# A delta-net projection that takes its input before the norm factor is known: where the factor is applied, and when waiting banks are evacuated

## The chip, the core and the metric

The kernel runs on one core of a Trainium2 chip. The metric is the device time of one execution in microseconds (us). Engines are named as in the profile: PE (TensorE's matmuls), PEld (its weight loads), DVE (VectorE), ACT (ScalarE), POOL (GpSimd), SP (SyncE, here a queue of DMAs); "q" behind a name is the engine's sequencer.

## The reference

The model has 256 tokens of width 1024 and two blocks. Only the first layer of the first block matters here:

```python
h = h + gated_deltanet(rmsnorm(h, a_norm_w), a_w_in, ...)
h = h + conv_gated_mlp(rmsnorm(h, ffn_norm_w), ...)
# gated_deltanet(hn, ...):
proj = hn @ w_in                      # q, k (8 heads), v, z (16 heads) of 128, gates b and a
qkv = silu(causal_dwconv(qkv, conv_w))        # width 4
q, k = l2norm(q) * 128**-0.5, l2norm(k)
beta = sigmoid(b); g = -exp(a_log) * softplus(a + dt_bias)
o = chunked_gated_delta_rule(q, k, v, g, beta)
o = rmsnorm(o, out_norm_w) * silu(z)
return o @ w_out
```

`rmsnorm` multiplies each token's row by its own factor (the inverse root of the mean square) and each column by a weight. The factor is one number for a token, so it can be applied to the input of a product or to its result.

## The kernel before, in words

One builder writes the whole program; a scheduler then orders each engine's instructions, the older ones first where several are ready. Activations lie transposed, 128 features by 256 tokens a tile. Each fp32 operand is split into a high and a low part, and each product of two tiles is three matmuls (`mm3`, lines 247 to 251): input high with weight high, input low with weight high, input high with weight low.

**Weights.** They lie in DRAM as 362 chunks of eight 128x128 tiles, in the order of use. `_raw` (line 168) loads a chunk through SP's queue, `_prep` (line 175) makes its high part on ACT (L186) and its low part on DVE (L187). `w` (line 230) hands out a tile, prepares two chunks ahead and, at every fourth tile, calls `tick`, which lets each waiting side task take one step. So a step is four tiles or twelve matmuls; side tasks count their delays in steps (`yield`).

**PSUM.** There are eight banks. `gemm` (line 257) fills a bank with two output tiles; with `ko=2` the first two banks are filled together, going through the eight input tiles once. A full bank goes to `evac` (line 207), which evacuates at once if `ready`, else keeps it in `evq`.

**The delta-net stage** (`gdn`, line 547, and `gdn_body`, line 576). The head loads the input in four parts (L519), squares it on ACT (L557), sums (L502, L558, L366), makes the factor (`rstd`, L379 and on), spreads it over a PSUM bank (`rows`, L418), and multiplies input, weight and factor on DVE (L568) before the split (L569, L570). `warm` (L554) puts products without use on PE in between. Weight chunk 0 is prepared meanwhile, chunks 1 and 3 behind given tiles of the input (`PINS`, through `behind`, line 192, which fixes an order on an engine).

Then the projection is multiplied: the first two banks of keys, the gates (`w_ba`, evacuated by `evac_ba`, line 609), two more banks of keys, and then blocks in the order of `ORDER` = "qqzqqzvvvvvvzvvz", where q is a bank of queries, v one of values, and z two banks of the output gate. In step numbers the keys end in step 18 and the last block in step 98.

- `conv` (line 646) evacuates a bank of k, q or v: for each of its two tiles one op on ACT (L651) and three on DVE (L654), then silu on ACT (L655). They read the bank itself.
- Nine steps later the squares of k or q are summed over features into bank `ssb` (L673).
- `x_stage` (line 701) waits for all four sums of keys and the gates, computes factors on DVE (`factors`, line 681), and then makes for eight pairs of heads key products (L707), decays (L711 to L715) and their product (L716); eight DMAs for each half (L722) take the result to DRAM.
- `inv_stage` (line 751) loads it back (L756) and inverts 32x32 blocks in 31 steps of two DVE ops (L764, L766), then sends results round again (L772 to L779).
- `levels` (line 865) joins the blocks to whole inverses (y1, z1, y2, z2), starting ten steps after the inversion with y1p (L832). `chain(q4)` (line 879) makes four heads' output: y0, x10, y1, o0, o1, then factor and gate on DVE (L929 to L937), a transpose (L945) and a split (L435, L436).
- The output projection `acc_k` adds up over 16 heads as they come.

Each of these is a side task; where the program has to wait for one without tiles to multiply, `until` (line 225) runs steps without products between them.

**Elsewhere.** `stats` (line 384) already does in the later norms what the change does here: the product starts, and the factor is applied at evacuation (L995 in the FFN). In `ffn2` (line 1685) `self.pins` holds the low parts of two chunks behind the DVE op that makes `dgx` (L1746), on which the products of L1760 depend.

Of the kernel before, what the change touches and what calls it, by code (L numbers as in the profile page):

```python
# [9 lines left out]
F32 = mybir.dt.float32  # L10
# [102 lines left out]
WARM = (5, 1, 3)  # L113
# [7 lines left out]
WSSB = 9  # L121
# [11 lines left out]
PRE0 = 1  # L133
# [5 lines left out]
PINS = {1: 0, 3: 1}  # L139
ORDER = "qqzqqzvvvvvvzvvz"  # L140


class Builder:
# [31 lines left out]
    def _prep(self, j):  # L175
# [12 lines left out]
        if j in self.pins:  # L188
            self.behind(i, self.pins[j])
# [67 lines left out]
    def gemm(self, name, x, K, ctiles, evac, ko=0):  # L257
# [170 lines left out]
    def split(self, hi, lo, src, scale=None, eng=None):  # L428

        nc = self.nc  # L430
        if scale is None:
            nc.scalar.activation(hi, src, AF.Copy)
            nc.vector.tensor_tensor(lo, src, hi.bitcast(F32), ALU.subtract)
# [71 lines left out]
    def run(self):  # L505
        nc, tc = self.nc, self.tc
        with ExitStack() as es:
# [9 lines left out]
            self.ident = self.cp.tile([P, P], F32, name="ident")  # L517
            for b in range(4):
# [4 lines left out]
            self.ones = self.cp.tile([P, P], F32, name="ones")  # L523
            nc.gpsimd.memset(self.ones, 1.0)
# [22 lines left out]
    def gdn(self):  # L547
# [3 lines left out]
        with tc.tile_pool(name="gp", bufs=1) as gp:  # L551

            wb = self.bank("warm")
            warm = lambda n, r: [nc.tensor.matmul(wb[:, 0 : r.shape[1]], self.ones, r, start=True, stop=True) for _ in range(n)]  # L554
            warm(WARM[0], self.ones)
            for b in range(4):
                self.add_sq(self.sqs, "sqa", b, lambda o: nc.scalar.activation(o, self.h[:, 2 * b : 2 * b + 2], AF.Square))  # L557
            nc.vector.tensor_tensor(self.sqs[0], self.sqs[0], self.sqs[1], ALU.add)  # L558
            cs = self.colsum(self.sqs[:1])
            if PRE0:  # L560
                self._prep(0)
            rc = self.rstd(cs, D)
            warm(WARM[1], self.sqs[0])
            rb = self.rows(rc, psum=True)
            warm(WARM[2], self.h[:, 0])
            for i in range(8):
                t = gp.tile([P, T], F32, tag="t2", bufs=8, name="xn")
# [8 lines left out]
    def gdn_body(self, gp, x):  # L576
# [32 lines left out]
        def evac_ba(g, b):  # L609
# [24 lines left out]
            def later():  # L634
                for _ in range(6):
                    yield
# [1324 lines left out]
```

## Time and profile before

| | us |
|---|---|
| median of three runs | 1212.6 (1211.88 to 1213.06) |
| the profiled execution, its own time | 1211.13 |
| its span, first to last instruction | 1209.3 |
| PE busy in the span | 1185.4 |
| DVE busy | 890.1 |
| ACT busy | 686.7 |

The profile is one execution. A row of a timeline gives the start, the length, engine and line, what is written from what, how often the instruction came in a row, and in brackets how long its engine was idle before it and what ended that. A row of groups gives busy time and the mean of one; matmuls overlap, so their pace is read from counts in a stretch, not from the mean. A row of windows gives for each engine its busy time and number of instructions in a stretch, then the granted clock's share, the DMA engines' share and GB/s.

### The profile page before, as it was taken

Reading aid. Unit: us, or ns where it says so; the run is one execution under the profiler, and the core shown is the slowest. Engines: PE = TensorE matmul, PEld = TensorE weight load, DVE = VectorE, ACT = ScalarE, POOL = GpSimd, SP = SyncE. Lnnn points to the kernel's source line nnn. Section 1 sums busy time; section 2 is a strip of 40 time slices with the busy share of each in tenths; the row PEclk is TensorE's granted clock in tenths of the full one; section 3 lists DMA queues with packets and bytes.
Section 4 is the critical chain, followed back from the end, with each engine's and each line's share of the span. In section 5 each row is a group of like instructions: output and inputs, shape, how many; then the busy total and the mean of one; then the engine's idle time right before and its main releaser. Section 6 shows DMA issues by size and latency. Waiting matters only on the chain.

```text
span 1209.3 us, 23369 instructions
## 1 busy us (share of the span) xinstructions
PE 1185.4 (98%) x9368; PEld 1122.7 (93%) x9368; DVE 890.1 (74%) x1642; ACT 686.7 (57%) x1166; POOL 20.4 (2%) x47
## 2 busy tenths in 40 slices
PE   6999999999999999999999999999999999999997
PEld 6989988999999999989999999889799999999996
DVE  6968977668877778879977878756656567655555
ACT  4786556556655556556655556754465455444443
POOL 1000000000000001000000000000000000000000
PEclk9999999999999999999999999999999999999999
DMA  6546385454655557434655655363255563555552
GB/s 212 187 134 201 120 223 178 140 165 155 208 187 180 188 178 248 131 102 149 206 185 184 192 183 165 116 201 123 88 174 175 176 241 119 180 185 184 188 181 82
DMA packets 68205, 206.00 MB, mean 170 GB/s; under 512 B 18086, under 2 KB 18230, under 8 KB 67841
## 3 DMA queue, kind: packets, MB, share of 16 engines
q1 hardware_dynamic: 65488, 194.77, 50.3%
q0 software_dynamic: 2608, 9.75, 2.3%
q8 instruction: 73, 1.20, 0.4%
q14 instruction: 36, 0.29, 0.1%
HBM read 199.75 MB, written 4.74 MB: 169 GB/s over the span
## 4 chain that ended last, share of the span: by engine, by line
PE 92%; DVE 5%; ACT 2%; issue 1%; DMA 0%; SPq 0%; DVEq 0%; ACTq 0%
PE pb L249 21%; PE pb L250 20%; PE pb L251 20%; PE acc L249 7%; PE acc L251 7%; PE acc L250 7%; DVE wl L187 1%; PE pt L1163 1%; PE ssb L673 1%; DMA ident<-cst 0%; DVE cy L654 0%; PE kv L1567 0%; ACT wh L186 0%; PE y1p L903 0%; PE csum L366 0%
## 5 line engine op out<-in xcount | busy, mean ns | idle before, releaser
L187 DVE TENSOR_TENSOR wl<-wr,wh 128x1024 fp32r<-128x1024 f32 x362 | 442.0, 1224 | 200.0 <-ACT wh L186 198.6
L186 ACT ACTIVATE wh<-wr 128x1024 fp32r<-128x1024 f32 x362 | 381.7, 1056 | 335.8 <-issue 99.3
L249 PE MATMUL pb<-xh,wh 128*128 128x256 f32 x1224 | 347.7, 284 | 0.6 <-ACT xh L569 0.6
L251 PE MATMUL pb<-xh,wl 128*128 128x256 f32 x1224 | 345.5, 283 | 0.7 <-DVE wl L187 0.7
L250 PE MATMUL pb<-xl,wh 128*128 128x256 f32 x1224 | 345.3, 282 | 0.2 <-DVE xl L570 0.2
L249 PEld LDWEIGHTS pb<-xh,wh 128*128 128x128 f32 x1224 | 231.6, 189 | 2.7 <-issue 1.3
L250 PEld LDWEIGHTS pb<-xl,wh 128*128 128x128 f32 x1224 | 230.3, 188 | 0.5 <-DVE xl L570 0.4
L251 PEld LDWEIGHTS pb<-xh,wl 128*128 128x128 f32 x1224 | 229.5, 188 | 0.9 <-DVE wl L187 0.9
L249 PE MATMUL pb<-fh,wh 128*128 128x256 f32 x416 | 118.4, 285 | 0.0
L250 PE MATMUL pb<-fl,wh 128*128 128x256 f32 x416 | 117.5, 283 | 0.1
L251 PE MATMUL pb<-fh,wl 128*128 128x256 f32 x416 | 116.7, 281 | 0.0
L249 PE MATMUL acc<-ah,wh 128*128 128x256 f32 x352 | 98.7, 280 | 0.0
L251 PE MATMUL acc<-ah,wl 128*128 128x256 f32 x352 | 98.6, 280 | 0.0
L250 PE MATMUL acc<-al,wh 128*128 128x256 f32 x352 | 98.5, 280 | 0.0
L249 PEld LDWEIGHTS pb<-fh,wh 128*128 128x128 f32 x416 | 77.9, 188 | 1.4 <-issue 0.4
L250 PEld LDWEIGHTS pb<-fl,wh 128*128 128x128 f32 x416 | 78.2, 188 | 1.1 <-DVE fl L436 0.3
L251 PEld LDWEIGHTS pb<-fh,wl 128*128 128x128 f32 x416 | 78.9, 190 | 0.0
L1002 DVE SCALAR_TENSOR_TENSOR fy<-fpad,cols,fy 128x256 f32<-128x256 f32 x176 | 73.6, 479 | 0.0
L249 PE MATMUL pb<-wh,xh 128*128 128x512 f32 (+1 forms) x176 | 70.3, 401 | 0.0
L250 PE MATMUL pb<-wl,xh 128*128 128x512 f32 (+1 forms) x176 | 68.2, 388 | 1.1 <-DVE wl L187 1.1
L251 PE MATMUL pb<-wh,xl 128*128 128x512 f32 (+1 forms) x176 | 67.9, 386 | 0.0
L249 PEld LDWEIGHTS acc<-ah,wh 128*128 128x128 f32 x352 | 66.8, 190 | 0.0
(438 smaller groups left out, 2082.7 us busy)
## 6 DMA issues: line engine op xcount, KB each, us to landing
wr<-wall SPq DMA_DIRECT2D x362, 512.0 KB, 3.6
wzd<-zt POOLq DMA_DIRECT2D x8, 256.0 KB, 2.9
wzog<-wzd POOLq DMA_DIRECT2D x4, 512.0 KB, 4.0
bias<-bd POOLq DMA_DIRECT2D x4, 512.0 KB, 7.4
h<-xT SPq DMA_DIRECT2D x4, 256.0 KB, 4.1
h<-xT POOLq DMA_DIRECT2D x1, 1024.0 KB, 7.6
wrow<-wrow POOLq DMA_DIRECT2D x1, 1024.0 KB, 9.0
out_dram<-mw SPq DMA_DIRECT2D x4, 256.0 KB, 2.0
```

The lines of the kernel that those rows point to most:

```text
L186: nc.scalar.activation(hi, r, AF.Copy)
L187: i = nc.vector.tensor_tensor(lo, r, hi.bitcast(F32), ALU.subtract)
L249: mm(out, ah, bh, start=start, stop=False, skip_group_check=skip)
L250: mm(out, ah, bl, start=False, stop=False, skip_group_check=skip)
L251: mm(out, al, bh, start=False, stop=stop, skip_group_check=skip)
L673: nc.tensor.matmul(ssb[:, c : c + 1], sq[:, i, tt * P : tt * P + P], self.ones[:, 0:1], start=True, stop=True)
L1002: nc.vector.scalar_tensor_tensor(y[:, i], u[:, i, j : j + T], w(j), y[:, i], ALU.mult, ALU.add)
L1163: nc.tensor.transpose(pt[:, j * P : j * P + P], S[:, i, j * P : j * P + P], self.ident)
```

## The change

- The input is split with its norm weight alone, as its parts land; the factor is made in a side task (`norm`) during the projection and applied at evacuation: by a new DVE op in `conv` (bank times row factor into `un`) and in `evac_ba`, and as the scale of z's copy.
- Banks wait in `evq` until the factor is there (step 14), and are then taken one every `NE` = 4 steps. The new op in `conv` is ordered behind the latest low part of weights on DVE.
- In the head input parts and weight chunks alternate on SP's queue; ident moves to POOL's queue, the norm weights come alone on ACT's, cols come last. ACT's and DVE's ops of the head are chained in written order. Thirteen products without use run ahead on PE.
- With `ko`, the products of one input tile are ordered by kind: all with both high parts, all with the input's low part, all with the weights' low part. This holds for all `gemm` calls with `ko`.
- A z block comes first in `ORDER`; delays of side tasks change; `x_stage`'s factors get a higher priority and three steps more; four of its last eight stores go to ACT's queue.
- `_prep` no longer looks into `self.pins`; `ffn2` still fills it.

```diff
-WARM = (5, 1, 3)
+WARM = 13
+NE = 4
+NA1, NA2 = 9, 4
-WSSB = 9
+WSSB = {"kss": 7, "qss": 9}
-PINS = {1: 0, 3: 1}
-ORDER = "qqzqqzvvvvvvzvvz"
+ORDER = "zqqzqqvvvvvvzvvz"
...
-        if j in self.pins:
-            self.behind(i, self.pins[j])
+        self.lastwl = i
...
             for k in range(K):
+                ts = []
                 for g in range(ko):
                     for i, c in enumerate(groups[g]):
-                        wh, wl = self.w(name, k * P, c * P)
-                        self.mm3(banks[g][:, i * T : i * T + T], wh, wl, xh[:, k], xl[:, k],
-                                 k == 0 and i == 0, k == K - 1, True)
+                        ts.append((banks[g][:, i * T : i * T + T], *self.w(name, k * P, c * P), k == 0 and i == 0))
+                for o, wh, wl, first in ts:
+                    mm(o, wh, xh[:, k], start=first, stop=False, skip_group_check=True)
+                for o, wh, wl, first in ts:
+                    mm(o, wh, xl[:, k], start=False, stop=False, skip_group_check=True)
+                for o, wh, wl, first in ts:
+                    mm(o, wl, xh[:, k], start=False, stop=k == K - 1, skip_group_check=True)
...
+            nc.scalar.dma_start(self.anw, self.a["cols"][:, 0:KD])
             for b in range(4):
                 nc.sync.dma_start(self.h[:, 2 * b : 2 * b + 2], self.a["xT"][:, 2 * b : 2 * b + 2])
-            nc.sync.dma_start(self.ident, self.cst("ident"))
-            self._raw(0)
+                if b < 3:
+                    self._raw(b)
+            nc.gpsimd.dma_start(self.ident, self.cst("ident"))
             nc.sync.dma_start(self.cols, self.a["cols"])
...
+            def tile_(i):
+                act.append(nc.scalar.activation(x[0][:, i], self.h[:, i], AF.Copy, scale=self.anw[:, i : i + 1]))
+                dve.append(nc.vector.scalar_tensor_tensor(x[1][:, i], self.h[:, i], self.anw[:, i : i + 1], x[0][:, i].bitcast(F32), ALU.mult, ALU.subtract))
+            def part(j, s):
+                r, hi, lo = raws[j], *self.halves[j]
+                act.append(nc.scalar.activation(hi[:, s], r[:, s], AF.Copy))
+                dve.append(nc.vector.tensor_tensor(lo[:, s], r[:, s], hi[:, s].bitcast(F32), ALU.subtract))
...
+            tile_(0)
+            part(0, lo)
+            tile_(1)
+            part(0, hi)
+            tile_(2)
+            tile_(3)
+            part(1, full)
+            s0 = square(0)
...
+            for l in (act, dve):
+                for p, n in zip(l, l[1:]):
+                    self.behind(n, p)
...
+            def norm():
+                for _ in range(NA1):
+                    yield
+                self.rc = self.sp.tile([P, 2], F32, tag="rc", bufs=1, name="rc")
+                self.rstd(self.colsum([s0[:, 0]]), D, None, self.rc)
+                for _ in range(NA2):
+                    yield
+                self.rb = self.rows(self.rc)
+                while self.evq:
+                    fn, args = self.evq.pop(0)
+                    fn(*args)
+                    for _ in range(NE if self.evq else 0):
+                        yield
+                self.ready = True
...
         def conv(bank, ct, dst):
+            un = t2([P, 2, T], "un")
+            self.behind(nc.vector.tensor_tensor(un, ev2(bank), self.bc2(self.rb), ALU.mult), self.lastwl)
             y = t2([P, 2, T], "cy")
             for i in range(2):
-                u = bank[:, i * T : i * T + T]
+                u = un[:, i]
...
-            factors(0)
+            with tc.high_priority(offset=60):
+                factors(0)
+            for _ in range(3):
+                yield
...
-                            Q[0].dma_start(s1[b, tt, H].rearrange("h s t -> s h t"), XA[blk(b), H, tt, blk(b)])
+                            (nc.scalar if j == 7 and tt else Q[0]).dma_start(s1[b, tt, H].rearrange("h s t -> s h t"), XA[blk(b), H, tt, blk(b)])
...
-            nc.scalar.activation(zt, b, AF.Copy)
+            nc.scalar.activation(zt, b, AF.Copy, scale=self.rc[:, tt : tt + 1])
```

In `evac_ba` one op more on 48 partitions multiplies the gates by the factor, and its `later` waits nine steps, not six. The two small ops `wfp` and `w1f` of `ffn(1)` (L1030, L1035), which the scheduler had moved to the head, are ordered behind the latest low part of an activation there, and identr (L591) behind the head's last DVE op.

## Rows read from the trace of the kernel before

**Rows 1.** The page, busy time of the engines.
```profile
PE 1185.4 (98%) x9368; PEld 1122.7 (93%) x9368; DVE 890.1 (74%) x1642; ACT 686.7 (57%) x1166; POOL 20.4 (2%) x47
```
**Rows 2.** Waits of PE, whole span: us in total, times, longest.
```profile
PE csum L366 <- DVE sqa L558: 6.6, 1, 6.6
PE acc L249 <- ACT oh L432: 2.0, 1, 2.0
```
**Rows 3.** Timeline of the head.
```profile
4.03 0.63 ACT L557 ACTIVATE sqa<-h 128x512 f32<-128x512 f32 x1 [2.02 <-DMA h<-xT]
...
7.73 0.63 ACT L557 ACTIVATE sq<-h 128x512 f32<-128x512 f32 x1 [1.07 <-DMA h<-xT]
...
10.07 1.01 PE L366 MATMUL csum<-ones,sqa 128*128 128x1 f32 x4 [6.58 <-DVE sqa L558]
...
15.98 0.50 PE L249 MATMUL pb<-xh,wh 128*128 128x256 f32 x2 [0.59 <-ACT xh L569]
```
**Rows 4.** Windows: us; PE, PEld, DVE, ACT, POOL busy (instructions); clock, DMA, GB/s.
```profile
300.00:400.00 100.00, 100.00 (x837) 100.00 (x836) 80.94 (x124) 57.89 (x86) 0.00 (x0) 1.00 0.58 187
```
**Rows 5.** Tiles bgp and y1p on PE: ns min/median/max, first and last start.
```profile
L639 PE MATMUL bgp<-ident,stk x2: 230/232/233, 41.6 to 41.6; 80*128 80x80 f32 x2
...
L832 PE MATMUL y1p<-h,XA x128: 191/191/212, 164.4 to 181.8; 32*32 32x32 f32 x128
```
**Rows 6.** Windows of the inversion, and from y1p to the stage's end.
```profile
105.60:152.60 47.00, 45.86 (x354) 44.01 (x353) 46.28 (x124) 26.19 (x42) 1.08 (x2) 1.00 0.47 147
...
164.40:272.00 107.60, 106.73 (x1200) 101.23 (x1200) 70.38 (x162) 61.96 (x142) 4.15 (x8) 1.00 0.53 170
```
**Rows 7.** Windows of the head, for the data rates.
```profile
2.00:4.00 2.00, 1.49 (x7) 1.20 (x6) 0.00 (x0) 0.01 (x1) 0.00 (x0) 1.00 0.87 222
4.00:6.00 2.00, 0.00 (x0) 0.00 (x0) 0.41 (x1) 1.26 (x2) 0.00 (x0) 1.00 0.93 321
6.00:8.00 2.00, 0.00 (x0) 0.00 (x0) 0.40 (x3) 0.90 (x2) 0.09 (x1) 1.00 0.97 347
```
**Rows 8.** Timeline of the head, products without use on PE.
```profile
0.99 2.50 PE L554 MATMUL warm<-ones 128*128 128x128 f32 x10 [0.99 <-POOL ones L524]
...
11.94 1.91 PE L554 MATMUL warm<-h,ones 128*128 128x256 f32 x4
...
14.79 0.60 PE L554 MATMUL warm<-h,ones 128*128 128x256 f32 x2
```
**Rows 9.** Timeline of PE, the first FFN's column sum.
```profile
280.33 0.95 PE L366 MATMUL csum<-ones,sqa 128*128 128x1 f32 x8
```
**Rows 10.** Groups of DVE in the first FFN, 272 to 480.
```profile
L1002 DVE SCALAR_TENSOR_TENSOR fy<-fpad,cols,fy 128x256 f32<-128x256 f32 x88 | 36.9, 479 | 0.0
L995 DVE TENSOR_TENSOR fpad<-pb,rowb 128x512 f32<-128x512 f32 x22 | 15.0, 689 | 8.0 <-PE pb L251 8.0
```
**Rows 11.** Groups of DVE during the inversion, 105.6 to 152.6.
```profile
L654 DVE SCALAR_TENSOR_TENSOR cy<-pb,cols,cy 128x255 f32<-128x255 f32 (+2 forms) x31 | 14.7, 475 | 0.3 <-ACT cy L651 0.3
L187 DVE TENSOR_TENSOR wl<-wr,wh 128x1024 fp32r<-128x1024 f32 x12 | 14.6, 1218 | 0.0
L766 DVE TENSOR_TENSOR TI<-TI,fst 128x31 f32<-128x31 f32 (+15 forms) x31 | 10.4, 336 | 0.2
```
**Rows 12.** Timeline of SP and DVE ahead of the inversion.
```profile
91.40 5.39 SPq L722 DMA_DIRECT2D s<-XA  x8
...
105.62 0.19 DVE L764 TENSOR_TENSOR fst<-NT,TI 128x31 f32<-128x31 f32 x1 [1.89 <-DMA NT<-s]
```
**Rows 13.** Timeline of DVE, factor and gating of the first chain.
```profile
201.21 0.16 DVE L929 TENSOR_TENSOR sc<-ms,rq 128x8 f32<-128x8 f32 x1
...
205.54 1.11 DVE L937 SCALAR_TENSOR_TENSOR wzog<-o1p,sc,wzog 128x128 f32<-128x128 f32 x4
```
**Rows 14.** Timeline of the last FFN's beginning.
```profile
1010.29 0.28 DVE L1746 TENSOR_SCALAR dgx<-ident,nrs 128x128 f32<-128x128 f32 x1
...
1010.63 0.60 PE L1760 MATMUL xt<-dgx,mw 128*128 128x128 f32 x3
```

More of the change, by code (lines that the diff above doesn't have):

```diff
@@ L432, in split @@
             nc.scalar.activation(hi, src, AF.Copy)
[L433 removed]
+            self.last = nc.vector.tensor_tensor(lo, src, hi.bitcast(F32), ALU.subtract)
         else:
@@ L553, in gdn @@
             wb = self.bank("warm")
[L554 to L567, printed above, removed]
-                op = nc.vector.scalar_tensor_tensor(t, self.h[:, i], self.col("a_norm", i), rb, ALU.mult, ALU.mult)
-                nc.scalar.activation(x[0][:, i], t, AF.Copy)
-                nc.vector.tensor_tensor(x[1][:, i], t, x[0][:, i].bitcast(F32), ALU.subtract)
-                if i in PINS:
-                    self.pins[PINS[i]] = op
-                    self._prep(PINS[i])
+            for _ in range(WARM):
+                nc.tensor.matmul(wb[:, 0:P], self.ones, self.ones, start=True, stop=True)
@@ new lines, in gdn @@
+            act, dve = [], []
+            act.append(nc.scalar.activation(self.sp.tile([P, 2], F32, tag="rky", bufs=2, name="tl"), self.ones[:, 0:2], AF.Square))
+            def tile_(i):
[5 more added lines that the diff above has]
+                dve.append(nc.vector.tensor_tensor(lo[:, s], r[:, s], hi[:, s].bitcast(F32), ALU.subtract))
@@ new lines, in square, with add, chunk @@
+            def square(b):
+                t = gp.tile([P, 2, T], F32, tag="t2", bufs=8, name="sq")
+                act.append(nc.scalar.activation(t, self.h[:, 2 * b : 2 * b + 2], AF.Square))
+                return t
+            def add(o, a_, b_):
+                dve.append(nc.vector.tensor_tensor(o, a_, b_, ALU.add))
+            raws = {}
+            def chunk(j):
+                self._raw(j)
+                raws[j] = self.raws.pop(j)
+                self.raws[j] = None
+                self.halves[j] = (self.wtile(j, F32R, "wh"), self.wtile(j, F32R, "wl"))
@@ new lines, in gdn @@
+            for j in range(3):
+                chunk(j)
+            lo, hi, full = slice(0, 512), slice(512, 1024), slice(0, 1024)
+            tile_(0)
[6 more added lines that the diff above has]
+            s0 = square(0)
+            tile_(4)
+            tile_(5)
+            s1_ = square(1)
+            chunk(3)
+            add(s0, s0, s1_)
+            part(2, full)
+            s2_ = square(2)
@@ new lines, in gdn @@
+            tile_(6)
+            tile_(7)
+            s3_ = square(3)
+            self._raw(4)
+            add(s0, s0, s2_)
+            part(3, full)
+            add(s0, s0, s3_)
+            add(s0[:, 0], s0[:, 0], s0[:, 1])
+            for l in (act, dve):
+                for p, n in zip(l, l[1:]):
+                    self.behind(n, p)
+            self.dvl = dve[-1]
+            self.ready = False
+            def norm():
[12 more added lines that the diff above has]
+                self.ready = True
@@ L574, in gdn @@
+            self.side(norm())
             self.gdn_body(gp, x)
@@ L590, in gdn_body @@
         nc.gpsimd.tensor_copy(identb, self.ident)
-        nc.vector.tensor_tensor(identr, self.ident[:, 32:48], self.ident[:, 64:80], ALU.add)
+        self.behind(nc.vector.tensor_tensor(identr, self.ident[:, 32:48], self.ident[:, 64:80], ALU.add), self.dvl)
         stk = gp.tile([P, T], F32, tag="stk", name="stk")
@@ L634, in later @@
             def later():
-                for _ in range(6):
+                for _ in range(9):
                     yield
@@ L667, in later @@
                 def later():
-                    for _ in range(WSSB):
+                    for _ in range(WSSB[key]):
                         yield
@@ L1029, in ffn @@
                 wfp = self.sp.tile([P, 8], F32, tag="wfp", bufs=1, name="wfp")
-                nc.vector.tensor_tensor(wfp, self.col("fin", 0, 8), self.col("prem", 0, 8), ALU.mult)
+                self.behind(nc.vector.tensor_tensor(wfp, self.col("fin", 0, 8), self.col("prem", 0, 8), ALU.mult), self.last)
                 xa = self.newx(tag="x")
@@ L1034, in ffn @@
                 nc.gpsimd.memset(w1f, 1.0)
-                nc.vector.tensor_tensor(w1f[:, :, 1], self.col("fin", 0, 8), self.col("fin", 0, 8), ALU.mult)
+                self.behind(nc.vector.tensor_tensor(w1f[:, :, 1], self.col("fin", 0, 8), self.col("fin", 0, 8), ALU.mult), self.last)
                 ev = self.boundary_evac([(xa, wfp)], w1f)
```

10 lines of the change are left out of this document (6 added, 4 removed).

## The prediction

> **What bounds the kernel now.** Read first the row of TensorE on the page [rows 1]: PE is busy for 1185.4 of a span of 1209.3 us, so time can only come from PE's idle time or from work taken off PE. The waits of PE show where that idle time is [rows 2]: 6.6 us of it is one wait, the column sum of the first norm waiting for the squares; no other wait is over 2.0 us. The timeline of the head shows the chain behind it [rows 3]: the four parts of the input are there at 4.03 to 7.73, squares and their sum take until 10.07, then column sum, rsqrt, row broadcast and the scaled input follow, and the first product of the projection runs at 15.98.
>
> I measure the head by one number, the time at which a projection without gaps would have had to begin. In undisturbed stretches PE does 837 products in 100 us [rows 4], 0.1195 us each. The kernel counts in steps: four weight tiles of three products, 1.434 us. The gates' transpose is issued in step 17, after 67 tiles, that is 201 products or 24.0 us; it runs at 41.6 [rows 5]. So the gap-free start is 17.6 us.
>
> After it PE hardly waits until the stage's last product at about 272.0, 107.6 us after the first product of the merge levels (y1p, 164.4 [rows 5]); of these 107.6 us PE is busy for 106.73 [rows 6]. DVE is the second limit: during the triangular inversion it is busy for 46.28 of 47 us [rows 6].
>
> **The change part by part.** My sum is made against the profiled execution, 1211.13 us; the median of the three runs is 1212.6, 1.5 above it, and I add that at the end.
>
> *Head.* The projection now needs only a part of the input and the first half chunk of weights. By the data rates [rows 7] some 0.44 MB have come in at 4 us, 1.09 at 6 and 1.78 at 8. In the new order on SP the first input part and the first chunk end at 0.79 MB, which is 5.1 us if transfers came strictly one after another. They don't: the whole input is 1.05 MB and was there at 7.73, not 5.9, since later transfers shared the engines; so 5.1 to 6.9, and I take 6.0. ACT's half chunk takes about 0.63 us (its 128x512 op [rows 3]), so operands are ready near 6.8. Thirteen warming products ahead of it on PE are 26 records of 0.25 us [rows 8], over at about 7.5 if all run as slowly as now. A chunk of 24 products lasts 2.87 us, while the next 0.77 MB (input part and chunk) come in 2.3 us at the 347 GB/s of [rows 7]: after the first chunk PE is the slower. All high-high products of four tiles come before those with low parts, so a low part has 1 us more. I take a gap-free start of 7.8 (6.8 to 9.7): **-9.8 us**. Squares, adds and the input's two parts (18 ops on ACT, 17 on DVE, each chained behind the one before it) lie beside these products. ident on POOL's queue, the small norm column on ACT's and cols behind the chunks on SP are used well after they land: nothing, or up to 1 us if cols delays the fourth chunk.
>
> *Norm inside the stream.* Column sum and row broadcast become four records each between products. Eight records of the one took 0.95 us [rows 9]; at that rate eight short ones cost a little less than a us: **+0.8** (0.5 to 1.2).
>
> *Waiting banks.* Each of the 16 q, k and v banks gets one more DVE op, bank times row factor, 128x512. The FFN has the same op at 689 ns [rows 10]: 11.0 us of DVE. The six convolution ops then read SBUF, not PSUM. The rows say that this gives nothing back: 479 ns from SBUF [rows 10], 475 from PSUM [rows 11]. The Trainium skill (VectorE: DVE Perf Modes, Rules for kernel authors) advises copying a product to SBUF first if many ops follow; by it the extra op would be repaid in part, and the next term would be near its lower end. I go by the rows.
>
> The banks also wait. The norm's side task makes the factor in step 14 and then takes a bank every four steps, about as fast as new ones come, so three stay behind. By the code the last key bank is evacuated in step 30 (now 18) and the x stage starts in step 39 (now 28): 11 steps, +15.8 us. With the head's -9.8, the norm's +0.8 and some -1.3 from splitting the last eight stores (5.39 us on SP) between two queues, the inversion starts 5.5 us later in the clock: 111.1 instead of 105.6 [rows 12]. Its higher priority for the factors I set against the three steps that it then waits.
>
> In its 47 us (105.6 to 152.6) DVE now does 12 low parts and 31 convolution ops, 29.3 us, and 31 ops of each of the inversion's two lines, 10.4 us a line [rows 11]. After, a bank falls on every four steps of the stretch: two low parts (2.44), six convolution ops (2.85) and the new op (0.69) are 6.0 us in 5.7 of products. Over 47 us, and with vtp's products between the steps, that is 7 groups or 42 us, 12 to 13 more than today, on an engine that is full. Some of it can wait (three chunks are prepared ahead, convolutions may fall behind the inversion): between 0 and 12 I take 7, the larger half because DVE's idle time there is 0.7 us [rows 6]. The new op is ordered behind the latest low part, so that one bank can't starve PE; what queues behind it on DVE is the convolution, and behind that the transposes of v.
>
> So the inversion ends at 111.1 + 47 + 7 = 165.1, and the levels start 11.8 later as now (152.6 to 164.4): 176.9. PE's own products end in step 98: now 164.4 is step 84, so side work to there is 164.4 - 17.6 - 120.5 = 26.3; after, 7.8 + 140.5 + 26.3 + 0.8 = 175.4. PE idles 1.5 us. From there, 107.6 less the 14 steps that no longer lie in between (20.1) are 87.5.
>
> *Lost cover.* Today the levels and the first chain run between z and v products. After, 16 steps of them stand alone before the output projection. On a chain DVE goes from 201.21 to 206.65 through factor and gating [rows 13], 5.4 us, with squares before it and transposes and a split behind; the next chain's products cover part of that. I take 4.0, below the 5.4 because of that cover; the bounds are 1 (covered but for short hops) and 9 (that path bare, and most of one more). The stage ends at 176.9 + 87.5 + 4.0 = 268.4, not 272.0: **-3.6 us**, all terms above included.
>
> *FFN at the end.* `_prep` no longer reads `pins`, which still holds two chunks of the last FFN behind `dgx`. PE takes up `dgx` at 1010.63, 0.06 us after DVE is done with it, and the low parts come behind it [rows 14]. If they slip in ahead, at 1.22 each [rows 11], PE waits up to 2.4; if the order stays, nothing. I take **+0.8**, nearer to the end at which the scheduler still puts the older work first. The other blocks with reordered products (both FFNs) have no wait there to lose; the two small ops of FFN 1's tail leave DVE's head: nothing.
>
> Sum: -3.6 + 0.8 = -2.8, so 1208.3 against 1211.1, and **1209.8** against the median. Other edits (identr, the gate block's scale) change an order or an operand and are taken at nothing; the pool of eight `t2` buffers, which the new op also uses, could add a wait, covered in the bounds.
>
> **The rivals.**
>
> *All of the head is kept.* If the inversion isn't delayed, y1p comes right behind the last product (175.4), and the lost cover is 1: the stage ends at 263.9, -8.1, so with +0.8 some 1205.3, or 1204.5 if the FFN costs nothing. For it: the inversion's older ops go ahead of later convolutions. Against it: DVE's 46.28 of 47.
>
> *Slower: DVE late before the levels.* The full 12 us and 7 of lost cover put the stage's end at 181.9 + 87.5 + 7 = 276.4, +4.4, and with +0.8 1217.8. It decides from the point where y1p starts after about 180. For it: DVE has no idle time left there. Against: before 105 it has some, into which deferred work could go.
>
> *The head starts late or slowly.* PE's records tell its clock: the same 128x256 form takes 0.48 us at 11.94 and 0.30 at 14.79 [rows 8], the lower and the higher level (1.2 and 2.4 GHz), with PE at work from 10.07 on. If first chunks land at 8 or come in spurts, two chunks at the low level cost 5.7 us and the gain is gone: 1213 to 1215. The Trainium skill (TensorE: Matmul & The Clock Gate, Part 1: The HAM clock gate) says that an array which waits for DMAs between short stretches of work swings between the two levels; the rows agree as far as 11.94 goes, and none shows it for the new order.
>
> *The change doesn't act as it says*: if the scheduler holds the new op behind low parts so long that banks run out (eight in all; three waiting, two or more in use), the stream itself stops; some 1214.
>
> **How the numbers follow.** A measurement of this kernel can tell about 0.2%, 2.4 us: faster is below 1210.2, slower above 1215.0. The forecast has 0.45 (1207.5 to 1212.5, of which 0.27 lies under 1210.2), all kept 0.20, DVE late 0.15, a late or slow head 0.12, the last with other mishaps 0.08. Faster: 0.27 + 0.20 + 0.03 = 0.50. Slower: 0.11 + 0.04 + 0.03 = 0.18. The same: 0.32. The range that leaves 2 in 10 out is 1204.0 to 1215.0.
>
> **What would show it.** Right: first projection product between 7 and 9 us, the last key bank's new op near 52; inversion from 110 to 113; y1p at 175 to 180; last product of the stage near 268; DVE full from about 110 to 175. Wrong: first product after 11 (head); inversion no longer than 48 us (all kept); y1p after 182 (slower); a PE gap over 1 us ahead of L1753 or L1760 (the FFN's term).

## The result and the profile after

The changed kernel takes **1222.4 us** (median of six runs, 1220.97 to 1225.43) where the kernel before takes 1212.2 beside it: a ratio of 1.0087 (95% interval 1.0076 to 1.0098), slower by about 10 us. Forecast were 1209.8 and a range of 1204 to 1215. The profiled execution took 1224.4, with a span of 1222.6.

The row of engines on the page, beside [rows 1]:
```profile
PE 1194.3 (98%) x9376; PEld 1130.0 (92%) x9376; DVE 895.1 (73%) x1652; ACT 695.4 (57%) x1175; POOL 20.9 (2%) x48
```
PE is busy for 8.9 us longer, with only eight products more. So the first question is not only where PE waits, but where it works slowly.

**The head came as forecast.** PE's timeline, where [rows 3] has the first product at 15.98:
```profile
3.71 1.98 PE L564 MATMUL warm<-ones 128*128 128x128 f32 x14
6.82 0.74 PE L270 MATMUL pb<-xh,wh 128*128 128x256 f32 x4 [1.13 <-ACT wh L575]
```
The norm's column sum runs at 21.47, behind 39 weight tiles (14.0 us): a gap-free start of 7.5, 10.1 earlier than before.

**The keys came late.** Tile kk on PE, of the kernel before and then of the changed one (ns min/median/max, first and last start):
```profile
L707 PE MATMUL kk<-kT x16: 377/378/462, 60.0 to 88.1; 128*128 128x256 f32 x16
```
```profile
L782 PE MATMUL kk<-kT x16: 377/378/631, 71.0 to 102.1; 128*128 128x256 f32 x16
```
Though the projection starts 10 us earlier by this measure, the first key product runs 11 us later, and the stage that it opens lasts 3 us longer.

**The inversion.** DVE's groups from its first op at 118.35 to its last at 174.8 (before: 105.6 to 152.6, [rows 11]):
```profile
L726 DVE SCALAR_TENSOR_TENSOR cy<-un,cols,cy 128x253 f32<-128x253 f32 (+2 forms) x44 | 20.7, 481 | 0.0
L187 DVE TENSOR_TENSOR wl<-wr,wh 128x1024 fp32r<-128x1024 f32 x14 | 17.1, 1222 | 0.0
L841 DVE TENSOR_TENSOR TI<-TI,fst 128x31 f32<-128x31 f32 (+15 forms) x31 | 10.6, 341 | 0.0
L839 DVE TENSOR_TENSOR fst<-NT,TI 128x31 f32<-128x31 f32 (+15 forms) x31 | 10.5, 339 | 5.0 <-DMA NT<-s 5.0
L718 DVE TENSOR_TENSOR un<-pb,rowb 128x512 f32<-128x512 f32 x7 | 4.8, 687 | 0.0
```
There are 44 convolution ops where 31 were, 14 low parts where 12 were, and 7 of the new op: from first op to last it is 56.4 us, before 46.8.

**The levels.** Tile y1p on PE, and PE's windows around it (columns as in [rows 4]):
```profile
L907 PE MATMUL y1p<-h,XA x128: 191/236/257, 185.5 to 202.7; 32*32 32x32 f32 x128
```
```profile
184.00:188.00 4.00, 2.78 (x14) 1.90 (x12) 3.11 (x7) 1.34 (x3) 0.00 (x0) 1.00 1.35 146
188.00:192.00 4.00, 2.55 (x103) 2.42 (x106) 3.38 (x8) 1.29 (x3) 0.00 (x0) 0.57 1.05 314
192.00:196.00 4.00, 2.88 (x71) 2.63 (x65) 3.75 (x9) 3.17 (x7) 0.00 (x0) 0.50 0.56 223
196.00:200.00 4.00, 3.26 (x70) 2.66 (x64) 0.96 (x2) 2.66 (x5) 0.00 (x0) 0.50 0.41 135
200.00:204.00 4.00, 4.00 (x120) 3.84 (x119) 3.89 (x8) 2.38 (x5) 0.00 (x0) 0.72 0.02 4
204.00:208.00 4.00, 4.00 (x101) 3.72 (x100) 1.96 (x4) 3.17 (x8) 0.54 (x1) 1.00 0.57 201
```
The last projection product is over at 186. Then the rest of y1p waits 2.2 us for its DMA, and with only short products left PE's granted clock is at 0.50, the lower level (1.2 GHz), from 188.6 to 202.2. The median of y1p is 236 ns, not 191. Before, the levels ran between projection products at a clock of 1.00 [rows 6].

**A budget for the stage.** The windows from 0 to the first FFN product, cut at 30, 120, 180 and 215, before and after:
```profile
0.00:30.00 30.00, 20.79 (x131) 18.60 (x132) 18.45 (x44) 14.49 (x23) 3.62 (x12) 1.00 0.62 211
30.00:120.00 90.00, 89.00 (x628) 81.82 (x628) 73.72 (x156) 64.12 (x119) 3.83 (x7) 1.00 0.56 176
120.00:180.00 60.00, 58.39 (x600) 54.03 (x600) 52.12 (x118) 33.72 (x57) 1.08 (x2) 1.00 0.59 167
180.00:215.00 35.00, 34.89 (x436) 31.07 (x433) 26.51 (x73) 24.32 (x64) 3.23 (x6) 1.00 0.53 189
```
```profile
0.00:30.00 30.00, 27.71 (x215) 27.28 (x216) 20.73 (x41) 19.03 (x30) 4.00 (x13) 1.00 0.82 289
30.00:120.00 90.00, 88.52 (x601) 80.63 (x600) 62.73 (x121) 65.59 (x116) 3.84 (x7) 0.98 0.49 156
120.00:180.00 60.00, 54.23 (x358) 47.77 (x357) 60.00 (x147) 34.76 (x55) 1.17 (x2) 1.00 0.45 147
180.00:215.00 35.00, 30.47 (x543) 26.99 (x542) 22.18 (x42) 19.57 (x42) 2.33 (x5) 0.80 0.72 188
```
I cut the same stretch into windows of 5 us and added up two things: PE's idle time, and its busy time multiplied by one less the granted clock, called lost clock here. What is left of the stage (rest) is PE's own work. All in us, the budget from one profiled execution each; the runs e1 to e18 follow below:

| kernel | stage ends | idle | lost clock | rest | median, ratio (95%) |
|---|---|---|---|---|---|
| before | 272.1 | 12.2 | 0.0 | 259.8 | 1212.2 |
| after | 282.6 | 15.1 | 7.0 | 260.4 | 1222.4, 1.0087 (1.0076 to 1.0098) |
| e1, all banks at once | 295.9 | 22.2 | 13.7 | 260.0 | 1232.5, 1.0174 (1.0156 to 1.0191) |
| e5, NE 2 | 284.3 | 16.9 | 8.3 | 259.1 | 1223.8, 1.0093 (1.0080 to 1.0107) |
| e2, without the new op | 275.2 | 10.2 | 7.2 | 257.8 | 1217.0, 1.0046 (1.0031 to 1.0060) |
| e7, before with the new op | 290.0 | 19.6 | 8.3 | 262.1 | 1230.4, 1.0144 (1.0129 to 1.0160) |
| e16, before, levels 14 steps later | 287.7 | 19.4 | 9.1 | 259.2 | 1228.9, 1.0132 (1.0117 to 1.0146) |
| e17, before, x stage 14 steps later | 286.1 | 19.3 | 7.0 | 259.8 | 1225.5, 1.0108 (1.0091 to 1.0124) |
| e18, input scaled from step 26 on | 287.0 | 15.6 | 12.7 | 258.7 | 1225.6, 1.0109 (1.0094 to 1.0124) |

PE's work is 258 to 262 us in all of them. The change takes 6.9 us of idle time out of the head (9.2 to 2.3 up to 30 us). Ahead of y1p it loses as much again: 5.1 more of idle time, most of it between 120 and 180, where PE waits for low parts and v's transposes, and 1.7 of clock (0.66 from 95 to 100). From y1p on it loses 5.6 of idle time and 5.4 of clock, where the kernel before lost 0.9 in all. So the 10.5 us at the stage's end are, but for 0.6 of rest, what the stretch from y1p on loses.

Of the 13.3 us between the two profiled executions the last FFN has 1.4 (below), and 1.4 lie between the stage's end and the last `csum`, where the clock from 500 to 550 is 0.94 in the changed kernel and 0.97 before. In e3 and e5, whose code there is the changed kernel's, it is 1.00.

### The profile page after: what moved, and what is told of

Its sections match the earlier page's. It is cut to its first block, busy times and chain, and to the rows that moved or that the text cites. A ratio compares the mean times of both kernels' runs of the same rounds, so it can differ in the third digit from the quotient of the medians.

```text
span 1222.6 us, 23425 instructions
## 1 busy us (share of the span) xinstructions
PE 1194.3 (98%) x9376; PEld 1130.0 (92%) x9376; DVE 895.1 (73%) x1652; ACT 695.4 (57%) x1175; POOL 20.9 (2%) x48
## 4 chain that ended last, share of the span: by engine, by line
PE 76%; DVE 2%; ACT 1%; issue 0%; DVEq 0%; ACTq 0%
PE pb L248 16%; PE pb L249 16%; PE pb L250 16%; PE acc L248 7%; PE acc L249 7%; PE acc L250 7%; PE pb L270 1%; PE pb L274 1%; PE pb L272 1%; PE pt L1238 1%; PE kv L1642 0%; PE gob L1659 0%; ACT S L1205 0%; DVE wl L187 0%; PE ms L1555 0%
## 5 line engine op out<-in xcount | busy, mean ns | idle before, releaser
L187 DVE TENSOR_TENSOR wl<-wr,wh 128x1024 fp32r<-128x1024 f32 x358 | 437.2, 1223 | 198.8 <-ACT wh L186 197.2
L186 ACT ACTIVATE wh<-wr 128x1024 fp32r<-128x1024 f32 x358 | 377.2, 1056 | 337.7 <-issue 95.8
L248 PE MATMUL pb<-xh,wh 128*128 128x256 f32 x1112 | 316.5, 285 | 0.7 <-DVE EA L815 0.7
L250 PE MATMUL pb<-xh,wl 128*128 128x256 f32 x1112 | 314.6, 283 | 1.1 <-DVE wl L187 1.1
L249 PE MATMUL pb<-xl,wh 128*128 128x256 f32 x1112 | 314.3, 283 | 0.0
L248 PEld LDWEIGHTS pb<-xh,wh 128*128 128x128 f32 x1112 | 210.8, 190 | 2.6 <-issue 1.3
L250 PEld LDWEIGHTS pb<-xh,wl 128*128 128x128 f32 x1112 | 209.1, 188 | 1.5 <-DVE wl L187 1.5
L249 PEld LDWEIGHTS pb<-xl,wh 128*128 128x128 f32 x1112 | 209.7, 189 | 0.1
```

The source lines that it names most:

```text
L186: nc.scalar.activation(hi, r, AF.Copy)
L187: i = nc.vector.tensor_tensor(lo, r, hi.bitcast(F32), ALU.subtract)
L248: mm(out, ah, bh, start=start, stop=False, skip_group_check=skip)
L249: mm(out, ah, bl, start=False, stop=False, skip_group_check=skip)
L250: mm(out, al, bh, start=False, stop=stop, skip_group_check=skip)
```

## The experiments

The expectations name theories by letters. L: the keys come late, and with them all that is counted in steps behind them. D: the 11 us of new work on a full DVE are the cost. C, later B: levels that run without projection products beside them ("bare") lose idle time and clock. F: the last FFN lost its order of low parts. S: a burst of evacuations holds back the weights' parts and starves the products. I: DVE has too much work inside the inversion's stretch. P: POOL slows DVE down. From e9 on, all runs of the changed kernel also have the FFN's order restored, as e3 has.

**How fast the banks are taken (e1, e5).**
```diff
-NE = 4
+NE = 0        # e5: NE = 2
```


> All waiting banks are evacuated in the step in which the factor is there (NE 0, not 4). Theory L (the keys come too late: the x stage, the inversion and the levels follow 14 steps behind, into the stretch in which DVE is full): the first key product moves from 71.0 to 45-50 us, the inversion starts at 97-104 instead of 118.4, y1p at 162-175 instead of 185.5, and the time falls to 1207-1213. Theory D (the 11 us of new DVE work are the cost, wherever the banks lie): y1p stays behind 180, time 1218-1223. Theory C (the clock's fall at 188-202 is the cost): it depends on whether PE still idles ahead of y1p.

> One waiting bank every two steps (NE 2, between 4 and the 0 of the run that took all banks at once). Theory S (a burst of evacuations holds the weights' two parts back on ACT and DVE, so that PE waits and its clock falls; spacing trades that against late keys): less PE idle time at 40-50 than the 2.35 us of the burst, inversion starts at 107-113, time 1216-1226, between or below 1222.4 and 1232.5. Theory L alone (late keys): inversion earlier by 6-10 us and the time 1213-1217. Rival D: y1p stays where it is (183-187), time 1221-1224.

L's times were wrong: the inversion did start at 107.6 and 107.0 instead of 118.4, but the kernels took 1232.5 and 1223.8. With all banks at once PE stands still for 2.35 us between 40 and 50, and its clock falls twice before 83 us:
```profile
40.00:50.00 10.00, 7.65 (x40) 5.84 (x39) 9.74 (x23) 9.05 (x14) 0.00 (x0) 1.00 0.00 1
...
70.00:80.00 10.00, 7.87 (x27) 6.21 (x28) 4.93 (x10) 9.69 (x30) 0.00 (x0) 0.62 0.12 46
```
DVE (9.74) and ACT (9.05) are full with banks, and no weights come in (1 GB/s). So S holds in that earlier keys are paid with late weight parts. Its other half failed: with a bank every two steps (e5) PE stands still for 2.86 us at 40 to 50, not for less than in e1.

**The new op alone, taken out and put in (e2, e7).**
```diff
-            un = t2([P, 2, T], "un")
-            self.behind(nc.vector.tensor_tensor(un, ev2(bank), self.bc2(self.rb), ALU.mult), self.lastwl)
...
-                u = un[:, i]
+                u = bank[:, i * T : i * T + T]
```
e2 leaves out the row factor of q, k and v, so its result is not the layer's; and its convolutions no longer wait for the factor (the first starts at 18.9 us, not 29.5). e7 does the reverse in the kernel before, with a tile of ones as factor, so there the op is alone.

> The convolutions read the bank itself: the 16 new DVE ops of 0.69 us and with them the row factor of q, k and v are left out (gates and z keep theirs). Theory D: with 11 us of DVE work gone the inversion (56.4 us) is back at 47-50, y1p comes 8-11 us earlier, time 1211-1214. Theory L: only the seven of these ops that lie inside the inversion count, 4.8 us at most, and the late start stays (inversion at 115-118); time 1217-1220.

> The kernel before with the new DVE op alone: each q, k and v bank is multiplied by a tile of ones into un, ordered behind the latest low part, and the convolutions read un. Head, order, banks and FFN stay. Theory D: 11 us of DVE work on a full engine delay y1p (164.4) by 5-11 us; the time is 1216-1221. Rival (DVE's idle 17 us between the first bank and the inversion take most of it): y1p 165-168, time 1212-1215.

Without op and wait it is 1217.0: L's time, but D's direction in the stage, where the inversion takes 52.1 us from 110.9 and y1p comes at 174.1 instead of 185.5. The levels are still bare, and 7.2 us of clock are lost. In the kernel before the 11 us of DVE work cost **18 us**, more than either theory gave: 7.4 more of idle time and 8.3 of clock. Half of that (7.9) lies between 30 and 90, where PE waits 2.8 us for the gates' transpose, with DVE late, and the clock from 40 to 50 is 0.77. Its levels are not bare:
```profile
L838 PE MATMUL y1p<-h,XA x128: 191/191/238, 175.0 to 196.1; 32*32 32x32 f32 x128
```
Their median is that of before, and 123 projection products are still to come at 175.0, as many as before at 164.4. So D holds, its price is not the op's duration, and it does not need B.

**The order in the last FFN (e3).**
```diff
+        if j in self.pins:
+            self.behind(i, self.pins[j])
         self.lastwl = i
```


> The check of self.pins in the weight preparation is restored, so that in the last FFN the low parts lie behind dgx again. Theory F (the FFN lost its order): the 1.7 us wait of PE at L1828 for DVE hn goes, time 1220.2-1221.0 where the changed kernel has 1222.4. Rival: the wait comes from something else (the stage before it, or the order of kinds), the row stays and the time is 1222-1223. Nothing before 1000 us moves under either.

The median is 1219.3 (1218.9 to 1220.9), the ratio 1.0062 (1.0050 to 1.0075), somewhat below the forecast. This row among the changed kernel's waits of PE behind 990 us is gone in e3:
```profile
PE xt L1828 <- DVE hn L1819: 1.7, 1, 1.7
```
From the last `csum` to the end it is 437.0 us before, 438.3 after, 437.0 in e3: F holds, and is 1.4 us. The rest of the 3.1 in the medians is not explained by it; in e3's execution the x stage lost no clock at 95 to 100, in that of the changed kernel it was 0.66 there.

**Products without use against the fall of the clock (e4, e8).**
```diff
-        self.until(lambda: st["A"] == 8)
+        fb = self.bank("fill")
+        while st["A"] < 8 or st["lev"] < 4:
+            for _ in range(1):
+                nc.tensor.matmul(fb[:, 0:P], self.ones, self.ones, start=True, stop=True)
+            self.tick()
```
e8 also puts one or two behind each group of the levels' own products.

> Some 12 products without use (24 records, about 3 us at the high level) run on PE between the last product of the projection and the rest of y1p, where the changed kernel idles 3 us and the granted clock falls to 0.50 from 188.7 to 202. Theory C: the granted clock stays at 1.00 there, the levels are 4-5 us shorter, time 1217.5-1219.5. Rival (the levels are a chain over ACT and DVE, PE's speed counts little, or the clock falls all the same): time 1221.5-1224.

> Products without use (128x128, 14 before and 17 between the merge levels' own products, about 7 us of PE) keep the whole array at work while the levels run alone. Theory C: the granted clock stays above 0.9 from 186 to 205, where it is 0.50 in the changed kernel, the small products take 191 ns and not 236 ns, and from y1p to the first transpose (otp) it takes 30-32 us and not 34.4: time 1218-1220.5. Rival: the products without use cost as much as the clock gives back, 1222-1226, or the clock falls all the same.

They took 1221.3 (ratio 1.0073, 1.0057 to 1.0089), not distinguishable from the changed kernel, and 1234.5 (1222.5 to 1235.0; 1.0155, 1.0123 to 1.0187). In e4's profiled execution, the slowest of six, the gap ahead of y1p is filled, and the clock falls all the same, some 4 us later:
```profile
186.00:190.00 4.00, 4.00 (x32) 3.68 (x31) 3.58 (x11) 0.91 (x2) 0.00 (x0) 1.00 1.24 154
190.00:194.00 4.00, 2.17 (x114) 1.85 (x113) 3.54 (x9) 2.92 (x7) 0.00 (x0) 0.86 1.03 402
194.00:198.00 4.00, 4.00 (x98) 3.73 (x98) 2.96 (x6) 3.17 (x7) 0.00 (x0) 0.50 0.29 92
198.00:202.00 4.00, 4.00 (x102) 3.57 (x102) 2.90 (x6) 1.95 (x4) 0.00 (x0) 0.50 0.38 130
```
In e8's profile too it is 0.50 from 190 to 200. But e8's six executions differ: the mean granted clock was 0.987 in the four that took 1234.5 to 1235.0 us, 0.992 in the one at 1229.3, and 0.999 in the one at 1222.5. So 12 us go with the clock there; and with the clock kept, the cover still only comes out level with the changed kernel (1222.4), the rival's case. That is one execution, and no profile shows its levels.

**Levels late in the kernel before, nothing else (e16, e17).**
```diff
-WINV = 10
+WINV = 24
```
e17 leaves that and puts `for _ in range(14): yield` ahead of `factors(0)` in `x_stage`.

> The kernel before with its levels issued 14 steps later (24 steps behind the inversion, not 10), so behind the last product of the projection as in the changed kernel; DVE's work and the head stay. Theory B: the granted clock falls to 0.5 in the levels and 7-12 us are lost to idle time and clock, time 1218-1224. Rival D (bare levels cost little, DVE's load is what counts): 1212-1215, with the granted clock at 1.00.

> The kernel before with one wait more: the x stage starts 14 steps later, as it does in the changed kernel (first key product in step 41, not 27). No new DVE work, the old head, the old order. Theory B with late keys (what is counted in steps behind the keys moves with them, the levels land behind the last product of the projection, PE idles there and its clock falls): first key product at 80-83, y1p at 185-195, granted clock 0.5 in the levels, time 1224-1232. Rival D (without the new DVE work the late stage is absorbed): 1212-1218.

e16's inversion ends where it did (TP at 152.5, before 152.9), its DVE work and its head are those of before; but y1p comes at 192.0 instead of 164.4, with six projection products left. It is 16.6 us slower, more than B gave. Windows of e16, beside the budget's of before, and its longest wait of PE between 120 and 195:
```profile
120.00:180.00 60.00, 55.67 (x385) 51.82 (x384) 52.22 (x116) 30.70 (x49) 1.08 (x2) 0.95 0.59 173
180.00:215.00 35.00, 31.11 (x511) 27.14 (x512) 15.00 (x24) 18.31 (x33) 2.16 (x4) 0.79 0.44 154
...
PE pb L249 <- ACT wh L186: 2.7, 1, 2.7
```
A part of it lies ahead of the levels: between 120 and 180 it loses 5.2 us more than the kernel before, in that wait for a weight chunk and the low clock behind it. e17 puts the keys' products behind as many steps as the changed kernel does (41), without the new op; y1p comes at 188.9, and it is 13.6 us slower, as B forecast. What each kernel loses from y1p to the stage's end, in idle time and lost clock, by the same windows of 5 us:

| kernel | y1p at, us | projection products left then | lost from there, us |
|---|---|---|---|
| before | 164.4 | 123 | 0.9 |
| after | 185.5 | 1 | 11.0 |
| e16 | 192.0 | 6 | 11.2 |
| e17 | 188.9 | 0 | 12.0 |
| e2 | 174.1 | 1 | 14.6 |
| e7 | 175.0 | 123 | 7.4 |
| e5 | 177.4 | 48 | 9.1 |
| e1 | 179.0 | 111 | 11.5 |

Levels moved to the end of the projection lose 10 to 11 us more than before, with the new op or without it, and that is the size of the changed kernel's whole loss: bare levels are enough for it, so far B holds. The other half of B, that cover would have saved it, is not shown: e1 and e5 have projection products left and lose nearly as much.

**Levels issued earlier (e13, e14, and e15 in the kernel before).**
```diff
-INVS = lambda j: True
+INVS = lambda j: j % 3 != 2
```


> The changed kernel with the FFN's order restored, and the inversion written out in 21 product steps, not 31 (three of its steps in every two), so that the levels are issued in step 90 and not 98, beside the last z block. Theory B (bare levels: behind the last product of the projection PE idles in their chain of short products and its clock falls to 0.50; 9.8 us of the changed kernel lie there): the granted clock stays above 0.9 from 175 to 210, PE's idle time and lost clock there are under 4 us, time 1211-1216. Rival D (DVE's work bounds the inversion's end at 172-175 however it is written out): PE waits for the levels ahead of the last z block, time 1217-1221.

> As the run before it, and on DVE the inversion's ops go ahead of convolutions, the weights' low parts ahead of both. Theory D with order (it is the convolutions queued ahead that hold the inversion up): inversion 44-48 us, time 1-3 us below the run before it. Rival: convolutions and with them v's transposes come late instead, PE waits for vtp, time equal or above.

> The kernel before with the inversion written out in 21 product steps. Theory B: its levels are covered already (granted clock 1.00, 0.4 us idle behind the inversion), so nothing is to be had: 1210.5-1213. Rival: an earlier inversion brings the whole stage forward, 1207-1210.

e14 also gives the inversion's ops on DVE priority over convolutions. All three were far slower: 1234.8 (1.0174, 1.0152 to 1.0195), 1238.3 (1.0204, 1.0187 to 1.0222), 1249.2 (1.0291, 1.0266 to 1.0315). In e13 and e15 all forecast times failed; in e14 the rival came true, with PE waiting 8.9 us for v's transposes (e13: 4.8). The first of PE's waits behind 120 us, in e13 and then in e15:
```profile
PE y1p L909 <- DMA h<-s: 7.7, 2, 4.7
```
```profile
PE y1p L832 <- DMA h<-s: 12.2, 1, 12.2
```
In e15 PE stands at y1p for 12.2 us, until 162.7, and none of the 192 projection products that stand behind it in the program runs meanwhile. So levels that stand ahead of projection products hold these up until the inversion's results are back, and the step number must fit the time at which DVE is done: too late is bare, too early is a stop. No run moves the changed kernel's levels by fewer steps than e13.

**Where DVE's work lies (e6, e18).** e6 sets `ORDER = "zqqqqvvvvvvvvzzz"`. e18 scales each input tile by the factor behind its last use in the first z block and keeps `un` for the keys only:
```diff
+                nc.vector.scalar_tensor_tensor(t, self.h[:, k], self.anw[:, k : k + 1], self.rb, ALU.mult, ALU.mult)
+                nc.scalar.activation(x[0][:, k], t, AF.Copy)
+                nc.vector.tensor_tensor(x[1][:, k], t, x[0][:, k].bitcast(F32), ALU.subtract)
```


> ORDER becomes z, four q, eight v, three z: the value banks' DVE work moves ahead of the inversion and the inversion lies beside z blocks, which need no DVE but for low parts. Theory I (DVE has 12 us too much work inside the inversion's stretch, and idle time ahead of it): the inversion takes 47-51 us instead of 56.4, y1p comes at 176-181, time 1214-1218. Rival D (the sum of DVE's work sets the inversion's end, wherever it lies): the x stage and the inversion's start move back by as much as the inversion gets shorter, y1p at 183-187, time 1220-1224.

> The changed kernel with the FFN's order restored, and the factor on the input again from step 26 on: while the first z block is multiplied, each input tile is scaled and split anew behind its last use there (16 DVE ops of about 0.45 us at 30-50); only the four key banks keep the new op, so 12 of 16 go. Theory D: 8 us of DVE work move from the late stretch to 30-50, the inversion takes 50-52 us, y1p comes at 176-181, time 1214-1218, between the run without the op (1217, less 2 for the FFN) and the changed kernel. Rival (DVE has no room at 30-50: keys and x stage come later still): first key product after 73, time 1219-1224. Theory B says of either that the levels stay bare and the clock falls there, so that it stays above the kernel before (1212).

e6: 1223.1 (1.0096, 1.0079 to 1.0113), y1p at 186.5: the rival's numbers, though not its way, for the inversion starts earlier (115.9) and is longer still (59.5 us). e18: 1225.6; the inversion takes 51 us as forecast, but the keys pay for it (first key product at 78.1, not 71.0), and y1p comes at 185.8: the rival's way, and above its time.

**DVE's work on POOL (e9 to e12).** e9 copies the bank on ACT and multiplies on POOL; e10, e11 (in the kernel before) and e12 (with NE 2) put every third low part there:
```diff
-            i = nc.vector.tensor_tensor(lo, r, hi.bitcast(F32), ALU.subtract)
+            pool = 8 <= j < 50 and j % 3 == 2
+            i = (nc.gpsimd if pool else nc.vector).tensor_tensor(lo, r, hi.bitcast(F32), ALU.subtract)
```


> The new op moves off DVE: ACT copies the bank to SBUF (16 more ACT ops of about 0.63 us) and POOL, idle until now, multiplies it there by the row factor; the FFN's order is restored (worth some 1.4-3 us). Theory D (the 11 us of new DVE work are what the change pays): inversion 49-53 us, y1p at 172-178, time 1211-1215. Rival (the late chain and the lost clock alone: the run that left the op out was still at 1217): 1214-1217. Rival P (POOL's op is several us long or slows DVE's two-input ops down, so that DVE is no freer): DVE's op for the convolution above 0.50 us, time 1219-1226.

> The changed kernel with the FFN's order restored and every third weight low part of chunks 8 to 49 (14 of 42) on POOL instead of DVE, 17 us of DVE work less. Theory D: the inversion takes 47-51 us, y1p comes at 172-180, PE idles less than 3 us from 120 to 180, time 1209-1214. Rival P: POOL is slow (above 4 us an op) or makes DVE's two-input ops longer, PE waits for the low parts instead: 1219-1230.

> The kernel before with the same 14 low parts on POOL. Theory D (DVE bounds the way to the levels in both kernels): PE has only 3 us of idle time behind the head to give back, so 1209.5-1212. Rival P: 1214-1225.

> As the run with low parts on POOL in the changed kernel, and one waiting bank every two steps. Theory S (what spoils faster evacuation is DVE and ACT being full while the banks are taken): with DVE relieved, the keys come earlier without starving PE; inversion starts at 103-108, time 2-5 us below the run with four steps. Rival: PE idles at 40-60 all the same (3 us and more, with its clock falling), time equal or above it.

They took 1231.5 (1.0161, 1.0146 to 1.0175), 1235.6 (1.0189, 1.0174 to 1.0203), 1219.6 (1.0059, 1.0045 to 1.0073) and 1237.5 (1.0201, 1.0185 to 1.0216). That is rival P in e9 to e11, in e9 and e10 with more than it gave, and the rival in e12, where PE idles 6.5 us between 40 and 60. e11's timeline, POOL and then DVE:
```profile
135.43 2.54 POOL L188 TENSOR_TENSOR wl<-wr,wh 128x1024 fp32r<-128x1024 f32 x1 [9.94 <-DVE cy L655]
```
```profile
135.64 0.48 DVE L655 SCALAR_TENSOR_TENSOR cy<-pb,cols,cy 128x254 f32<-128x254 f32 x1
136.03 2.19 DVE L767 TENSOR_TENSOR TI<-TI,fst 128x231 f32<-128x231 f32 x1
138.14 0.47 DVE L655 SCALAR_TENSOR_TENSOR cy<-pb,cols,cy 128x253 f32<-128x253 f32 x1
```
While POOL subtracts (until 137.97), DVE's op with both inputs in SBUF takes 2.19 us, not 0.4, and ends 0.25 us behind POOL's; the op that reads the bank keeps its 0.48.

No version here beats the kernel before.

## Why the prediction was wrong

**Right**: the head (7.5 for 7.8), the new op (16 at 0.676 to 0.694 us), that reading SBUF gives nothing back (convolution ops 479 ns, before 475), the last stores (last XA to the load of NT: 7.8 us before, 6.5 after), and what DVE would find in the inversion: 42 ops of convolution, 14 low parts and 7 new ops were forecast, 44, 14 and 7 came. The FFN's term is 1.4 where I took 0.8 of at most 2.4.

**Wrong**, in the order of the steps:

1. *"11 steps, +15.8 us" for the x stage.* In the program's order the first key product moved from step 27 to step 41: 14 steps, 20.1 us. The three steps added behind the factors, which I had "set against" their priority, count in full. With 3 us more for the stage itself, in which DVE waits 11.8 us for ACT's exponentials instead of 6.5, the inversion starts at 118.4 and not at 111.1.
2. *"Between 0 and 12 I take 7."* The inversion became 9.6 longer; inside the bounds. With a last step that is 1.1 shorter than taken, y1p stands at 185.5 instead of 176.9.
3. *"PE's own products end in step 98 ... 175.4."* They ended at 186. I let DVE delay the inversion and put at nothing what the same full DVE does to low parts and v's transposes: PE idles 5.8 us between 120 and 180 (before 1.6), 2.8 of it for low parts and 1.7 for these transposes.
4. *"I take 4.0 ... the bounds are 1 and 9"* for the lost cover. From y1p to the end it is 97.1 us, 9.6 more than the 87.5 of work, and outside the bounds: 5.6 of idle time and 5.4 of lost clock, where the same stretch before had 0.9 of idle time. The term was mis-sized because I counted only DVE's path and no clock. That the clock could fall I had asked of the head alone, where it didn't matter; the stretch that I had just stripped of its projection products was the place for the question. The Trainium skill (TensorE: Matmul & The Clock Gate, Part 1: The HAM clock gate) says that an array which waits between short stretches of work swings between its two levels. The rows from 184 to 200 agree as far as they go: PE waits for 0.7 to 1.5 of each 4 us there, and the clock falls, once. e4's rows, with PE busy for all of 194 to 202 at 0.50, show that waits are not all that kept it low.

So the stage ends at 282.6 instead of 268.4: 8.6 of the 14.2 us lie ahead of y1p and 5.6 behind it. The rival that came true is "DVE late before the levels": it decides, as said, with y1p after 180. I gave it 0.15 and 1217.8, short of the truth because it kept my start of the inversion and my bounds for the cover. Its way is only a part of what happened: of the 8.6 us, 7.3 are the inversion's late start and 2.6 its length, and the last step gave 1.1 back. The early start reached PE's products alone: the first key bank's convolution begins on DVE at 30.8 us, behind `un` at 28.7, and began at 30.6 before. So the change moved the end of the projection towards a chain that had become later.

The prices of the single parts do not add up to the loss: late keys alone cost 13.6 (e17), the op alone 18 (e7), op and wait for the factor taken out give back 5.4 (e2), the head gives 6.9 of idle time. They overlap where they open the same gap, bare levels. But that is not all that they do: e7's loss does not need bare levels.

## What to carry to other kernels

An earlier start of the engine that bounds is worth something only if the chain that joins it later starts earlier too; ask first what the new time lets begin, and what still waits for the same thing as before. Where side work is placed by counting steps of the main stream, a delay early on moves all of it towards the stream's end: check whether the last of it still has main work beside it, and price a bare stretch with its clock as well as its waits. Main work that is left over is not yet cover (e1, e5). An op added to a full engine costs what it makes others wait for, which was 1.6 times its own length in the kernel before.

## What was not expected of the hardware

- A stretch in which PE is busy for 2.6 to 4.0 of each 4 us, mostly with 32x32 and 64x64 products, ran at a granted clock of 0.50 for 13.7 us (188.6 to 202.2), while the same products between 128x256 ones kept 1.00 before. Twelve products without use ahead of them only moved the fall (e4).
- POOL's 128x1024 subtraction takes 2.40 us on average in e11 and 2.56 in e10 (DVE 1.22), and DVE's ops with two inputs in SBUF stand still meanwhile: in e11 their longest takes 2.53 us, against 0.4. In e10 the convolution ops, which there read `un` in SBUF, average 598 ns from 60 to 190 us; in e11, where they read the bank, 476 from 60 to 170. The Trainium skill (GPSIMD Engine Reference, 1. Specifications) says that POOL shares its SBUF interfaces with VectorE, with contention for instructions with two SBUF inputs. The trace agrees: the longest takes 2.53 us where the bank's reader keeps its 0.48.
